# One more plain pair of gate and up in the last three feed-forward layers

## The chip, the cores and the metric

The kernel runs on one core of one Trainium2 chip. The metric is device time in microseconds (us) of one execution; lower is better. A profile of one execution shows when each engine was busy: PE multiplies matrices (PEld is its loading of the stationary operand), DVE and ACT are the two engines for elementwise work, POOL is a third that here mostly issues transfers, and SP issues the other transfers. Each engine takes its own instructions in the order in which they were written into its queue and stops at the first whose inputs are not there.

## The reference, cut to what matters

Two layers, each a half-step feed-forward network (FFN), a mixer, and a second half-step FFN. The change touches the FFN alone, and three of its four uses.

```python
def swiglu(h, w_in, w_out):
    g, u = jnp.split(h @ w_in, 2, axis=-1)
    return (jax.nn.silu(g) * u) @ w_out

for i in range(DEPTH):                       # DEPTH = 2
    h = adaln(x, norm_g[i, 0], shift[:, 0], scl[:, 0])
    x = x + HALF * gate[:, 0, None, :] * swiglu(h, ffn_w_in[i, 0], ffn_w_out[i, 0])
    ...
    h = adaln(x, norm_g[i, 2], shift[:, 2], scl[:, 2])
    x = x + HALF * gate[:, 2, None, :] * swiglu(h, ffn_w_in[i, 1], ffn_w_out[i, 1])
```

There are 512 tokens, 1024 model features and 2816 hidden features; everything is float32.

## The kernel before

All activations are kept transposed, features on 128 partitions and tokens along the row, so `x` is eight tiles of 128x512. A float32 operand is split into a high part (a copy on ACT, line 170) and a low part (a subtraction on DVE, line 171), and each product is made of three matmuls, high by high, low by high and high by low (`mm3`, lines 179 to 181).

The 2816 hidden features are 22 column blocks of 128, numbered j. For one j the kernel needs a gate block and an up block, here called a pair. There are two ways of making a pair:

- Plainly (`pair`, line 423): gate and up each take 8 slices of the model features, so 2 x 8 products over all 512 tokens. A product over 512 columns is three matmuls of 128x512, or, with the tokens in two halves (`HALVES`), six of 128x256. In halves a pair is 2 x 8 x 2 x 3 = 96 matmuls of 128x256.
- By seven products (`seven_products`, line 488), a scheme after Strassen and Winograd: the 2 x 2 arrangement of gate and up by first and second half of the features is multiplied with the 2 x 2 arrangement of features by tokens in seven products instead of eight. Each of the seven covers 4 slices of features and 256 tokens, so a pair is 7 x 4 x 3 = 84 matmuls of 128x256.

Seven products need sums of weight quarters. For each j, SP loads two quarters into a buffer `qa` (lines 500 and 501), POOL adds a third to both with an accumulating transfer (line 503, it waits for the first two), SP loads the whole gate block into `raw` (line 505) and one quarter into `a22` (line 506; the profile's page calls it `a`). DVE makes two more sums `qb` (lines 507 and 508), and then everything is split into high and low: `raw` to `whi`, `qa` to `qah`, `a22` and `qb` to `qbh`. On PE the products follow in the order a11, a12, s3, s1, a22, s2, s4; a11 and a12 use `whi`, s3 and s1 use `qah`, the last three use `qbh`. Between a11 and s1 ACT copies the first product away (`p1`, line 530; `p` on the page), because s1 is summed into the same place. DVE and ACT then put the products together (lines 536 to 543).

The seven products also need sums of the activations' quarters. `quarters` (line 326) makes them once per FFN from the normalized input, after the norm is finished: four passes on DVE, and four splits into the tiles `th` and `tl`. That takes time, so the first pairs of an FFN are made plainly from the unsummed input. In `ffn` (line 479) these are j = 0 and 1, which are worked together as soon as the norm delivers (`head_start`, PE tile `hs`), and j = 2 (line 559), whose gate weights lie in the tiles that `th` takes afterwards. From j = 3 on `seven_products` is used.

The buffers that matter: `qa` has two buffers of its own, called `own` here, and two more are made of the tiles `hhi1` and `hlo1` (line 564), which hold the first half of the features over the second half of the tokens and are read by plain pairs alone, so they come free when the last plain pair is done. The order of use is own, own, own, `hhi1`, `hlo1`, own, own, and so on. So the third j that is made by seven products takes the first one's buffer again, the fourth waits for the plain pairs. `qah` and `qal` have two buffers, `qbh` and `qbl` one.

The hidden blocks are used up in four parts, `FOUR` = 0 to 6, 6 to 12, 12 to 18 and 18 to 22: after each part the output projection (PE tile `y`) multiplies them with `ffn_w_out` and adds the result to `x`.

The code is written in the order of the computation; a scheduler at build time then fixes the order of the instructions in each engine's queue by priorities and its own estimates. The queues are static: at run time nothing overtakes within one.

Of the kernel before, what the change touches and what calls it, by code (L numbers as in the profile page):

```python
# [24 lines left out]
T = 512  # L25
# [24 lines left out]
HALVES = ((0, HT), (HT, T))  # L50
# [3 lines left out]
def decoder_kernel(ctx, tc, xT, cT, ng, adaw, adab, ffi, ffo, cwi, cw, cwo,  # L54
# [8 lines left out]
    def shift(p, n):  # L63
        p.tile([P, n // 4], F32, name="shift")
# [12 lines left out]
    def psum(name, tag="mm"):  # L77
        tag = next(six) if tag == "mm" else {"pr": "o"}.get(tag, tag)
        return ps.tile([P, T], F32, name=name, tag=tag, bufs=2)
# [35 lines left out]
    def mod(s, kind, d):  # L115
        c = s * NMOD + kind * KD + d
        return mods[:, c:c + 1]
# [65 lines left out]
    def weights(src, nk, ncol, own=None, held=3, raws=None, to=None, added=False):  # L183
        def part(name, dt, bufs, from_):
            return (from_ or wp).tile([P, nk * ncol], dt, name=name, tag=name, padded_shape=[P, KD * P], bufs=bufs)

        hi, lo = to or (part("whi", F32R, held, own), part("wlo", F32R, held, own))
        raws = raws or own
        raw = part("wraw", F32, 3 if raws in (None, wp) else 2, raws)
        nc.sync.dma_start(raw.rearrange("p (a n) -> p a n", a=src.shape[1]), src)  # L190
        if added:
            split_added(raw, src, hi, lo)
        else:
            split(raw, hi, lo)
        return [t.rearrange("p (k n) -> p k n", n=ncol) for t in (hi, lo)]


    def project(o, w, wc, h, ks, first, last, a=0, b=T):
        c = slice(wc * P, (wc + 1) * P)
        for n, (kw, k) in enumerate(ks):  # L200
            mm3(o, w[0][:, kw, c], w[1][:, kw, c], h[0][k][:, a:b], h[1][k][:, a:b],
                first and n == 0, last and n == len(ks) - 1)
# [193 lines left out]
    def ffn_in(f, j, c, own=None):  # L396
        return weights(ffi[f, j, c], KD, P, own)


    def ffn_out(f, d, m, j0, j1, own=None):  # L400
        src = ffo[f, d:d + m, :, j0 * P:j1 * P].rearrange("d p c -> p d c")
        return weights(src, m * (j1 - j0), P, own)
# [17 lines left out]
            nc.vector.tensor_mul(af, sg, u)  # L420
            self.keep(af)

    def pair(f, j, h, own=None, gate=None):
        gu = []
        for c in range(2):
            w = gate if gate and not c else ffn_in(f, j, c, own if c else None)
            o = psum("gu")
            for a, b in HALVES if gate else ((0, T),):
                project(o[:, a:b], w, 0, h, [(k, k) for k in range(KD)], True, True, a, b)
            gu.append(o)  # L430
        return gu
# [3 lines left out]
    def ffn_first(s, f, nrm, nxt, extra, ahead, first, soon, own):  # L435
        with ExitStack() as es:
# [23 lines left out]
            for p, (j0, j1) in enumerate(PARTS):  # L460
                for j in range(max(j0, nj), j1):
                    hid.activate(*pair(f, j, h, own))
                    fill()
                n = j1 - j0
                a, ka = (hid.hi[j0:j1], hid.lo[j0:j1]), [(k, k) for k in range(n)]
                last = p == len(PARTS) - 1
                for d in range(KD - 3 if last else KD):
                    w = ffn_out(f, d, 1, j0, j1, own if d % 2 else None)
                    o = psum("y")
                    project(o, w, 0, a, ka, True, True)  # L470
                    if last:
                        residual(s, d, o, nxt)
                    else:
                        fill()
                        nc.vector.scalar_tensor_tensor(x[d], o, mod(s, 2, d), x[d], op0=ALU.mult, op1=ALU.add)
# [3 lines left out]
    def ffn(s, f, nrm, nxt, w0, ahead):  # L479
        with ExitStack() as es:  # L480
            hp = pool(es, "hp", 1)
            hid = Hidden(es, 12)
            keep = hid.keep
            nj = 2
# [64 lines left out]
            with ExitStack() as tf_es:  # L549
                nrm.alloc_seven(hp, pool(tf_es, "tf", 1))  # L550
                h = nrm.hi, nrm.lo
                with ExitStack() as hw_es:
                    hw = pool(hw_es, "hw", 1)
                    shift(hw, 64)
                    w = w0 + [weights(ffi[f, j, c], KD, P, hw, 1, wp) for j, c in js[len(w0):]]

                    gate = weights(ffi[f, nj, 0], KD, P, to=[tt.tile([P, D], F32R, name="w" + e, tag=f"t{e}1") for e in "hl"])
                    os = head_start(nrm, h, [(lambda k, w=w_: (w, 0, k)) for w_ in w])
                os += pair(f, nj, h, gate=gate)
                nrm.quarters(tt)  # L560
            nj += 1
            sw_es = es.enter_context(ExitStack())

            own, quarter = (partial(swa.tile, [P, 2, KD * P // 2], F32, name="qa", bufs=2),
                            [partial(hp.tile, [P, 2, KD * P // 2], F32, name="qa", tag=t) for t in ("hhi1", "hlo1")])
            sums = chain((own, own, own), cycle((*quarter, own, own)))
            sw = pool(sw_es, "sw", 1)
            shift(sw, 64)
            for j in range(nj):
                hid.activate(os[2 * j], os[2 * j + 1])  # L570
            for p, (j0, j1) in enumerate(FOUR):
                for j in range(max(j0, nj), j1):
                    seven_products(j)
                n = j1 - j0
                a = (hid.hi[j0:j1], hid.lo[j0:j1])
                if p < len(FOUR) - 1:
                    for d in range(KD):
                        w = ffn_out(f, d, 1, j0, j1)
                        o = psum("y")
                        project(o, w, 0, a, [(k, k) for k in range(n)], True, True)  # L580
                        nc.vector.scalar_tensor_tensor(x[d], o, mod(s, 2, d), x[d], op0=ALU.mult, op1=ALU.add)  # L581
# [663 lines left out]
    ada_es.close()  # L1245
    nrm, nxt = nxt, Norm(3)
    w = ffn(2, 1, nrm, nxt, w, ffn_ahead(2))
    nrm, nxt = nxt, Norm(4)
    w = ffn(3, 2, nrm, nxt, w, lambda: nsa_in(4))
    nrm, nxt = nxt, Norm(5)  # L1250
    w = nsa(4, nrm, nxt, w, ffn_ahead(3))
    ffn(5, 3, nxt, None, w, None)


# [73 lines left out]
```

## Time and profile before

| | us |
|---|---|
| three runs | 1984.94, 1996.69, 1997.26 (median 1996.69) |
| the profiled execution, its own time | 1994.45 |
| span of the profile, first to last instruction | 1992.4 |
| DVE busy | 1471.6 (74%) |
| ACT busy | 886.4 (44%) |
| POOL busy | 212.3 (11%) |

The profiled execution's time is 2.05 us more than its span and 2.24 us under the median of the runs. The three FFNs that `ffn` makes begin their first pair by seven products at 612.79, 965.93 and 1678.08 us of the span; they are called the first, second and third FFN below. A share of busy time is an average over the whole span; what a change in one place is worth is read in that place.

### The profile page before, as it was taken

How to read it: one execution, taken by the hardware profiler on the slowest of the kernel's cores; microseconds unless marked ns; L12 is line 12 of the kernel's file. 1: busy time of each engine (PE TensorE's matmuls, PEld its weight loads, DVE VectorE, ACT ScalarE, POOL GpSimd, SP SyncE). 2: the span in 40 equal slices, each digit the busy share in tenths (PEclk: the TensorE clock that was granted, in tenths of full speed). 3: DMA queues.
4: the chain of work that ended last, by engine and by line, in shares of the span. 5: the costliest groups of instructions: out<-in, count | busy, mean ns of one | idle time of the engine just before them, and what ended most of it. 6: DMA issues, size and time to landing. Idle time of an engine off the chain costs nothing.

```text
span 1992.4 us, 32482 instructions
## 1 busy us (share of the span) xinstructions
PE 1924.9 (97%) x12644; PEld 1746.8 (88%) x12644; DVE 1471.6 (74%) x2581; ACT 886.4 (44%) x1426; POOL 212.3 (11%) x295
## 2 busy tenths in 40 slices
PE   5999999999998999999999999999999889999999
PEld 4878888898898898999989899999888789898989
DVE  7878888674467586778768677885776877786865
ACT  3322322332245353435535343456887955343532
POOL 0000000100011000000100000002354620000000
PEclk9999999999998999999999999999998999999999
DMA  8888999422236464533656553146233424665622
GB/s 310 304 317 318 329 323 331 155 98 85 89 102 186 132 175 142 155 117 96 183 135 176 142 154 117 45 139 169 66 68 76 112 64 114 172 173 156 170 69 75
DMA packets 115350, 315.78 MB, mean 158 GB/s; under 512 B 14139, under 2 KB 14411, under 8 KB 115196
## 3 DMA queue, kind: packets, MB, share of 16 engines
q1 hardware_dynamic: 97164, 274.81, 40.8%
q0 software_dynamic: 18032, 38.90, 11.5%
q8 instruction: 99, 1.62, 0.3%
q14 instruction: 55, 0.45, 0.1%
HBM read 310.51 MB, written 3.15 MB: 157 GB/s over the span
## 4 chain that ended last, share of the span: by engine, by line
PE 72%; DVE 11%; DMA 9%; ACT 5%; issue 3%; SPq 1%; DVEq 0%; ACTq 0%
PE gu L179 10%; PE gu L181 10%; PE gu L180 10%; DMA adaraw<-in_adaw 6%; PE y L179 6%; PE y L180 6%; PE y L181 6%; DVE wlo L171 2%; DVE adaraw L125 2%; PE hs L179 2%; PE hs L181 2%; PE hs L180 2%; PE cv L181 2%; PE cv L179 2%; PE cv L180 2%
## 5 line engine op out<-in xcount | busy, mean ns | idle before, releaser
L170 ACT ACTIVATE whi<-wraw 128x1024 fp32r<-128x1024 f32 (+2 forms) x271 | 268.9, 996 | 501.0 <-PE y L180 223.3
L171 DVE TENSOR_TENSOR wlo<-wraw,whi 128x1024 fp32r<-128x1024 f32 (+2 forms) x271 | 309.4, 1144 | 53.9 <-ACT whi L170 52.0
L179 PE MATMUL gu<-hhi,whi 128*128 128x256 f32 (+1 forms) x808 | 257.8, 319 | 0.0
L181 PE MATMUL gu<-hhi,wlo 128*128 128x256 f32 (+1 forms) x808 | 257.7, 319 | 0.0
L180 PE MATMUL gu<-hlo,whi 128*128 128x256 f32 (+1 forms) x808 | 257.7, 319 | 0.0
L179 PE MATMUL y<-ahi,whi 128*128 128x512 f32 x587 | 228.4, 392 | 0.8 <-ACT ahi L170 0.7
L180 PE MATMUL y<-alo,whi 128*128 128x512 f32 x587 | 227.5, 390 | 0.4 <-DVE alo L171 0.4
L181 PE MATMUL y<-ahi,wlo 128*128 128x512 f32 x587 | 227.1, 389 | 0.0
L125 DVE CUSTOM_DVE_ANT_0 adaraw<-adaraw,cond 128x1024 f32<-128x1024 f32 x144 | 174.6, 1223 | 34.6 <-DMA adaraw<-in_adaw 32.8
L179 PEld LDWEIGHTS gu<-hhi,whi 128*128 128x128 f32 x808 | 151.7, 188 | 12.3
L180 PEld LDWEIGHTS gu<-hlo,whi 128*128 128x128 f32 x808 | 151.6, 188 | 12.2
L181 PEld LDWEIGHTS gu<-hhi,wlo 128*128 128x128 f32 x808 | 151.7, 188 | 11.8
L503 POOL DMA_DIRECT2D qa<-in_ffi x57 | 68.7, 1204 | 818.5 <-DMA qa<-in_ffi 163.1
L179 PE MATMUL gu<-th,qah 128*128 128x256 f32 x456 | 129.1, 283 | 13.0 <-ACT p L530 13.0
L179 PEld LDWEIGHTS y<-ahi,whi 128*128 128x128 f32 x587 | 109.5, 188 | 27.8 <-ACT ahi L170 5.0
L180 PEld LDWEIGHTS y<-alo,whi 128*128 128x128 f32 x587 | 110.2, 188 | 24.9 <-DVE alo L171 2.5
L181 PEld LDWEIGHTS y<-ahi,wlo 128*128 128x128 f32 x587 | 110.2, 188 | 22.7
L179 PE MATMUL gu<-th,qbh 128*128 128x256 f32 x456 | 126.1, 277 | 3.2 <-ACT qbh L170 3.2
L180 PE MATMUL gu<-tl,qah 128*128 128x256 f32 x456 | 128.5, 282 | 0.0
L181 PE MATMUL gu<-th,qal 128*128 128x256 f32 x456 | 128.4, 282 | 0.0
L581 DVE SCALAR_TENSOR_TENSOR x<-y,mods,x 128x512 f32<-128x512 f32 x72 | 54.0, 750 | 98.7 <-PE y L181 98.6
L180 PE MATMUL gu<-tl,qbh 128*128 128x256 f32 x456 | 125.9, 276 | 0.0
(308 smaller groups left out, 5243.0 us busy)
## 6 DMA issues: line engine op xcount, KB each, us to landing
adaraw<-in_adaw SPq DMA_DIRECT2D x144, 512.0 KB, 5.9
wraw<-in_ffi SPq DMA_DIRECT2D x119, 512.0 KB, 4.1
qa<-in_ffi SPq DMA_DIRECT2D x114, 256.0 KB, 4.0
qa<-in_ffi POOLq DMA_DIRECT2D x57, 512.0 KB, 6.4
wraw<-in_ffo SPq DMA_DIRECT2D x72, 384.0 KB, 4.3
a<-in_ffi SPq DMA_DIRECT2D x57, 256.0 KB, 4.3
wraw<-in_cwi SPq DMA_DIRECT2D x24, 512.0 KB, 3.3
wraw<-in_nwi SPq DMA_DIRECT2D x20, 512.0 KB, 4.3
```

The source lines that it names most:

```text
L125: nc.vector.tensor_tensor_reduce(out=raw, in0=raw, in1=cond, scale=1.0, scalar=0.0, op0=ALU.mult, op1=ALU.add, accum_out=m)
L170: nc.scalar.activation(hi, src, AF.Copy)
L171: nc.vector.tensor_tensor(lo, src, hi, ALU.subtract)
L179: nc.tensor.matmul(o, sh, mh, start=first, stop=False)
L180: nc.tensor.matmul(o, sh, ml, start=False, stop=False)
L181: nc.tensor.matmul(o, sl, mh, start=False, stop=last)
L503: nc.gpsimd.dma_start(qa, bass.AP(tensor=a21.tensor, offset=a21.offset, ap=[a21.ap[0], [0, 2], a21.ap[1]]), accum_op=ALU.add)
L581: nc.vector.scalar_tensor_tensor(x[d], o, mod(s, 2, d), x[d], op0=ALU.mult, op1=ALU.add)
```

## The change

The three FFNs that `ffn` makes get a fourth plain pair. j = 3 is made by `pair`, in halves like j = 2, and is activated with the others; `seven_products` starts at j = 4, so eighteen j are made by it instead of nineteen. Nothing else is edited.

```diff
-    def pair(f, j, h, own=None, gate=None):
+    def pair(f, j, h, own=None, gate=None, halves=False):
         gu = []
         for c in range(2):
             w = gate if gate and not c else ffn_in(f, j, c, own if c else None)
             o = psum("gu")
-            for a, b in HALVES if gate else ((0, T),):
+            for a, b in HALVES if gate or halves else ((0, T),):
                 project(o[:, a:b], w, 0, h, [(k, k) for k in range(KD)], True, True, a, b)
             gu.append(o)
         return gu
...
                 os += pair(f, nj, h, gate=gate)
                 nrm.quarters(tt)
-            nj += 1
             sw_es = es.enter_context(ExitStack())
...
-            for j in range(nj):
+            for j in range(nj + 1):
                 hid.activate(os[2 * j], os[2 * j + 1])
+            hid.activate(*pair(f, nj + 1, h, halves=True))
+            nj += 2
             for p, (j0, j1) in enumerate(FOUR):
                 for j in range(max(j0, nj), j1):
                     seven_products(j)
```

The scheduler's order around this place changes with it. Numbers behind names tell buffers apart. First the queue of ACT in the first FFN, before the change, from the first j by seven products (j = 3, whose quarter is `a22_5098`) to the second (j = 4, `a22_5223`, `p1_5260`); `qa_5347` is that of the third, j = 5.

```order
L170 ACTIVATE qbh_5102<-a22_5098 128x512
L170 ACTIVATE qah_5350<-qa_5347 128x1024
L170 ACTIVATE qbh_5227<-a22_5223 128x512
L170 ACTIVATE qbh_5227<-qb_5224 128x1024
L530 ACTIVATE p1_5260<-gu_5246 128x256
```

The same queue with the change. `ahi_5208` belongs to the new plain pair, `a22_5216` and `p1_5253` to j = 4, `a22_5341` and `p1_5378` to j = 5, and `qa_5673` to j = 6.

```order
L170 ACTIVATE ahi_5208<-af_5206 128x512
L530 ACTIVATE p1_5253<-gu_5239 128x256
L170 ACTIVATE qbh_5220<-a22_5216 128x512
L170 ACTIVATE whi_5488<-wraw_5490 128x768
L170 ACTIVATE qah_5676<-qa_5673 128x1024
L170 ACTIVATE qbh_5345<-a22_5341 128x512
L170 ACTIVATE qbh_5345<-qb_5342 128x1024
L530 ACTIVATE p1_5378<-gu_5364 128x256
```

In both, the split of the third `qa` stands ahead of the second `p1`; with the change that third `qa` is the one of j = 6, a j of the next part.

Then SP's queue of transfers in the first FFN, before the change. `qa_5805` and `qa_5680` take the tiles `hlo1` and `hhi1`, `qa_5347` is the third, `a22_5098` the quarter of the first j by seven products.

```order
L190 DMA wraw_5471<-in_ffo 128x768
L500 DMA qa_5805<-in_ffi 128x512
L500 DMA qa_5680<-in_ffi 128x512
L500 DMA qa_5347<-in_ffi 128x512
L506 DMA a22_5098<-in_ffi 128x512
L506 DMA a22_5223<-in_ffi 128x512
L501 DMA qa_5347<-in_ffi 128x512
```

With the change; here `qa_5923` and `qa_5798` take `hlo1` and `hhi1`, `qa_5673` is the third, `a22_5216` the quarter of the first j by seven products.

```order
L190 DMA wraw_5464<-in_ffo 128x768
L500 DMA qa_5673<-in_ffi 128x512
L501 DMA qa_5673<-in_ffi 128x512
L190 DMA wraw_5490<-in_ffo 128x768
L500 DMA qa_6048<-in_ffi 128x512
L501 DMA qa_6048<-in_ffi 128x512
L190 DMA wraw_5516<-in_ffo 128x768
L500 DMA qa_5923<-in_ffi 128x512
L500 DMA qa_5798<-in_ffi 128x512
L506 DMA a22_5216<-in_ffi 128x512
L506 DMA a22_5341<-in_ffi 128x512
```

Both quarters of the third `qa`, two weight blocks of the output projection and one more `qa` have moved ahead of the two transfers that wait for the last plain pair; the quarters `a22` of the first and second j stay behind them. With the change the other two FFNs have the same two pieces in the same order. Elsewhere the queues differ only where neighbouring instructions have changed places, at the norms and in the mixer of the second layer.

## The prediction

> **What bounds the kernel now.** I read the page's first part, then who PE waits for, then a table of stretches cut at the pairs, and last the queues of ACT and SP at the places found. The first row is PE's busy time in the page, the other two are from the list of waits on PE (waiter, what it waited for, us in total, times, longest).
>
> ```profile
> PE 1924.9 (97%) x12644; PEld 1746.8 (88%) x12644; DVE 1471.6 (74%) x2581; ACT 886.4 (44%) x1426; POOL 212.3 (11%) x295
> ```
> ```profile
> PE gu L179 <- ACT p L530: 13.0, 4, 6.9
> ...
> PE gu L179 <- ACT qbh L170: 3.2, 2, 1.8
> ```
>
> PE bounds the kernel at 97%, so a matmul more costs its time, and time comes back only where PE stands. The longest waits inside the FFNs are for the copy `p1` and the split `qbh`, both of the seven products. Now the stretches. Columns: from:to in us, length, then busy time of PE, PEld, DVE, ACT and POOL with their counts, PE's granted clock, busy share of the DMA engines, GB/s. The first row is the plain pair j = 2 of the second FFN; then come j = 3, 4 and 5 by seven products, of the first, second and third FFN.
>
> ```profile
> 954.85:965.93 11.08, 11.08 (x97) 11.08 (x96) 9.95 (x12) 7.54 (x10) 0.00 (x0) 1.00 0.29 86
> 612.79:623.25 10.46, 10.06 (x87) 9.86 (x86) 9.05 (x12) 4.43 (x7) 2.39 (x2) 1.00 0.91 292
> 623.25:642.66 19.41, 12.52 (x87) 12.32 (x85) 9.89 (x14) 5.84 (x8) 2.39 (x2) 0.74 1.03 244
> 642.66:652.28 9.62, 9.62 (x86) 9.62 (x85) 7.55 (x10) 5.04 (x7) 1.20 (x1) 1.00 0.53 130
> 965.93:977.82 11.89, 10.08 (x87) 9.69 (x85) 6.76 (x9) 3.48 (x6) 2.41 (x2) 1.00 0.96 272
> 977.82:991.61 13.79, 11.41 (x86) 11.21 (x85) 10.21 (x14) 5.75 (x8) 2.41 (x2) 0.88 1.04 249
> 991.61:1001.13 9.52, 9.52 (x86) 9.52 (x85) 7.93 (x12) 4.93 (x7) 1.20 (x1) 1.00 0.88 249
> 1678.08:1689.55 11.47, 10.08 (x87) 9.70 (x85) 6.69 (x9) 3.52 (x5) 2.39 (x2) 1.00 0.95 271
> 1689.55:1704.40 14.85, 11.57 (x87) 11.37 (x86) 10.34 (x15) 5.74 (x8) 2.39 (x2) 0.89 1.01 234
> 1704.40:1714.02 9.62, 9.62 (x86) 9.62 (x85) 7.81 (x11) 4.94 (x7) 1.19 (x1) 1.00 0.89 258
> ```
>
> A pair by seven products takes 9.52 us when PE never stands (84 matmuls, 113.3 ns each). j = 3 and j = 4 take much more, j = 5 almost nothing: over 9.52 us the first FFN loses 0.94 + 9.89 + 0.10, the second 2.37 + 4.27 + 0, the third 1.95 + 5.33 + 0.10. That is 10.93 + 6.64 + 7.38 = 24.95 us. At the same time the DMA engines are busy for 0.91 to 1.04.
>
> j = 4 loses in two ways. In the next table each wait is followed by the stretch behind it.
>
> ```profile
> 626.07:633.12 7.05, 0.16 (x2) 0.00 (x0) 1.75 (x3) 2.84 (x5) 0.00 (x0) 0.65 1.11 252
> 633.12:638.41 5.29, 5.29 (x24) 5.29 (x25) 5.25 (x9) 1.95 (x3) 1.19 (x1) 0.50 0.93 179
> 980.54:983.08 2.54, 0.16 (x2) 0.00 (x1) 1.75 (x2) 2.49 (x4) 0.98 (x1) 1.00 1.11 256
> 983.08:987.53 4.45, 4.45 (x24) 4.45 (x25) 4.38 (x8) 1.59 (x3) 1.43 (x2) 0.62 1.09 255
> 1692.27:1695.71 3.44, 0.16 (x2) 0.00 (x0) 1.75 (x2) 2.79 (x4) 0.00 (x0) 1.00 1.11 266
> 1695.71:1700.16 4.45, 4.45 (x25) 4.45 (x25) 4.38 (x8) 1.59 (x3) 2.23 (x2) 0.62 0.86 193
> ```
>
> PE stands for 7.05, 2.54 and 3.44 us, and its next 24 matmuls then run at a granted clock of 0.50 to 0.62: 5.29, 4.45 and 4.45 us where 24 x 113.3 ns are 2.72. So 6.03 us of the loss are slow matmuls after a wait. Why PE stands is in ACT's queue, first FFN, then one row each of the second and the third.
>
> ```profile
> 617.40 0.63 ACT L170 ACTIVATE qbh<-a 128x512 fp32r<-128x512 f32 x1 [0.64 <-DMA a<-in_ffi]
> 630.28 1.06 ACT L170 ACTIVATE qah<-qa 128x1024 fp32r<-128x1024 f32 x1 [12.25 <-DMA qa<-in_ffi]
> 631.24 0.61 ACT L170 ACTIVATE qbh<-a 128x512 fp32r<-128x512 f32 x1
> 631.76 1.04 ACT L170 ACTIVATE qbh<-qb 128x1024 fp32r<-128x1024 f32 x1
> 632.71 0.36 ACT L530 ACTIVATE p<-gu 128x256 f32<-128x256 f32 x1
> 632.97 0.83 ACT L170 ACTIVATE whi<-wraw 128x768 fp32r<-128x768 f32 x1
> ```
> ```profile
> 980.24 1.06 ACT L170 ACTIVATE qah<-qa 128x1024 fp32r<-128x1024 f32 x1 [6.95 <-DMA qa<-in_ffi]
> ```
> ```profile
> 1692.87 1.06 ACT L170 ACTIVATE qah<-qa 128x1024 fp32r<-128x1024 f32 x1 [7.85 <-DMA a<-in_ffi]
> ```
>
> ACT stands at the split of j = 5's `qa`, whose transfer has not landed, and the `p1` that PE wants for j = 4 is four places behind it. That `qa` is the third: its buffer had to be given back by j = 3 first. It lands 17.49, 14.31 and 14.79 us after the start of j = 3.
>
> **The change part by part.** Write T for the end of the new plain pair, which is the start of j = 4.
>
> *The pair and the j that goes.* Per FFN 96 matmuls come and 84 go. The priced row is the plain pair above, 11.08 us (at 113.3 ns each it would be 10.88), against 9.52: +1.56 us, three times +4.68 us, all on PE's path. On ACT and DVE the pair needs two weight splits, one gate and one product with its split, less than the seven products' 4.93 us of ACT and 7.93 of DVE in 9.52; I cost them at nothing, covered by the 11.08 us of PE. Its weights are loaded and split in the places that j = 3's and j = 4's blocks had before.
>
> *The third `qa`.* It now belongs to j = 6, which comes after the output projection of part 0. Its split still stands ahead of the `p1` of j = 5 in ACT's queue. PE wants that `p1` at T + 9.52 + 2.72 = T + 12.24 (two products of 1.36 in), and it was ready 632.71 + 0.36 - 630.28 = 2.79 us after the landing, so landings up to T + 9.4 are free. Landing at the same clock time as before would be T + 6.4, T + 3.2 and T + 3.7, since T is 11.08 later than the start of j = 3 was; and SP now issues its two quarters together and ahead of the `a22` group. So the 7.05, 2.54 and 3.44 us go, and the slow matmuls with them.
>
> *The `a22` of the first j.* SP stands at the two `qa` loads that need the `hhi1` and `hlo1` tiles, and the `a22` loads are queued behind. The rows for the third FFN: SP's issues, then ACT's split of the arrived quarter, and last, over all 57, how long this transfer takes.
>
> ```profile
> 1676.80 0.95 SPq L500 DMA_DIRECT2D qa<-in_ffi  x2
> 1677.80 0.42 SPq L501 DMA_DIRECT2D qa<-in_ffi  x1
> 1678.33 0.37 SPq L500 DMA_DIRECT2D qa<-in_ffi  x1
> 1678.75 0.90 SPq L506 DMA_DIRECT2D a<-in_ffi  x2
> ```
> ```profile
> 1684.39 0.63 ACT L170 ACTIVATE qbh<-a 128x512 fp32r<-128x512 f32 x1 [2.65 <-DMA a<-in_ffi]
> ```
> ```profile
> DMA to landing us min/median/max: 2.5/4.3/11.2
> ```
>
> The first load was let go at 1676.80, 12 matmuls before the plain pairs' end, and `a22` was issued 0.67 us after that end and landed 5.64 us later, so PE got `qbh` late: that is j = 3's loss. In the new order only the two freed loads stand ahead (0.95 us), so `a22` goes at about T - 0.4. PE wants it after four products, T + 5.44, and ACT needs 0.63 before: a landing 5.2 us after the issue is free. At 5.64 us PE loses 0.43, and 0.9 for the low part on DVE; at 4.3 nothing. I take 0.5 us per FFN, 1.5.
>
> *What is left of the loss.* In the first FFN even an undisturbed j ran at 9.62; I leave 0.8 us for such slower matmuls. With 1.5 that is 2.3 of 24.95.
>
> *Transfers.* From the page's list of issues (engine, count, size, median us to landing):
>
> ```profile
> wraw<-in_ffi SPq DMA_DIRECT2D x119, 512.0 KB, 4.1
> qa<-in_ffi SPq DMA_DIRECT2D x114, 256.0 KB, 4.0
> qa<-in_ffi POOLq DMA_DIRECT2D x57, 512.0 KB, 6.4
> wraw<-in_ffo SPq DMA_DIRECT2D x72, 384.0 KB, 4.3
> a<-in_ffi SPq DMA_DIRECT2D x57, 256.0 KB, 4.3
> ```
>
> A plain pair loads 2 x 512 KB, a seven-product j 256 + 256 + 512 + 512 + 256: 768 KB less in each burst, not priced. Two weight blocks for the output projection move ahead of the waiting loads on SP; two issues take about the 0.95 us of the row above, at a time when SP would otherwise wait for PE. What stands behind the waiting loads (`a22`, later weights, POOL's sums for j = 7 and 8) is wanted after T + 5.
>
> *Sum.* 24.95 - 2.3 - 4.68 = 18.0 us. Against the profiled execution's own time 1994.45 that is 1976.5; it stands 2.24 under the median 1996.69, so against the median 1978.7. I say 1979.
>
> **A rule beside the row.** The rows show half to 0.62 of the clock behind waits of 2.54 to 7.05 us. The Trainium skill, TensorE: Matmul & The Clock Gate, Part 1, says that PE falls to half rate after an idle window of about 3.4 us and comes back after as long a busy one. By that each wait costs 1.7 us more, 5.1 us for three, where the rows give 6.03; the sum by the page would be 17.1 us. The trace agrees with the half rate and the length; that a wait of 2.54 us sufficed is the trace's, and it decides.
>
> **The rivals.**
>
> *The wait stays and moves along.* If j = 6's `qa` lands as late after T as j = 5's did after the start of j = 3, only j = 3's and j = 5's losses go, 0.94 + 2.37 + 1.95 + 0.20 = 5.46, less 4.68: 0.8 us faster, 1995.9. For it: ACT's order is unchanged. Against it: the load waits for a split on DVE that needs nothing of the new pair, and stands ahead of SP's wait.
>
> *`a22` later than thought.* Everything that waited for the plain pairs is still issued in one burst at T. If its landing takes 7.5 us, PE stands 2.3 us per FFN and pays about 2.0 for the slow clock (6.03 / 3): 24.95 - 0.8 - 4.68 - 12.9 = 6.6 us faster, 1990. From 10 us on, 4.8 + 2.0 each, the gain is gone, and at the longest seen, 11.2, it is 6.0 + 2.0 each, 24 us: 4.5 us slower, 2001. Against it: 11.2 is one of 57, and much of the old burst is now issued before T.
>
> *Nothing lost at all.* The pair at 10.88 and no loss left: 20.9 us, 1975.8.
>
> **How the numbers follow.** The waits go with only small rests (1979, including the last rival): 0.72. `a22` at 6.5 to 10 us: 0.14, about 1990. The wait moves along: 0.08, 1996. `a22` over 10 us: 0.04, 2001. Shifts elsewhere in the order that overshadow this: 0.02. The three runs lie 12.3 us apart, and the median of new ones can fall among the lower; so the likeliest case alone is 1969 to 1986, and the range that leaves out 2 in 10 is 1967 to 1991. About 1% is what a measurement of this kernel can tell from no change, and that bound, 1976.7, lies just under the forecast: of the likeliest case I give 0.34 to below it. So faster 0.34, the same 0.63, slower 0.03.
>
> **What would show it.** In the profile afterwards: PE's wait for `p` gone from the list or under 1.5 us in total; j = 4 and 5 at 9.5 to 10.3 us each with a clock of 1.00; the new pair at 10.9 to 11.1; 36 matmuls more; from the start of the new pair to the output projection about 30.9 us where before it was 39.49, 35.20 and 35.94. The prediction is wrong if ACT again stands at a `qah` ahead of `p`, if `qbh` is late by more than 1 us, or if the time comes back in a later part of the FFNs.

## The result, and the profile after

| | before | after |
|---|---|---|
| median of the runs first taken | 1994.42 us (6 runs, 1984.94 to 1997.26) | 1972.6 us (6 runs, 1968.97 to 1982.23) |
| ratio after to before | | 0.991, 95% interval 0.989 to 0.993 |
| the same pair on another chip | 1990.58 us (9 runs) | 1978.27 us (5 runs, 1975.92 to 1981.09) |
| ratio there | | 0.9938, interval 0.9922 to 0.9953 |
| profiled execution | 1994.45 us, span 1992.4 | 1970.97 us, span 1969.2 |

The kernel became faster by 21.8 us in the first comparison and by 12.3 in the second, by the medians; 18.0 had been forecast. By the intervals of the ratios the gain is 14 to 22 us in the first and 9 to 16 in the second. A difference near 1% is at the edge of what is measured here, so the two traces have to say where it comes from. First PE's line of the page after, and what PE waits for:

```profile
PE 1918.0 (97%) x12680; PEld 1739.8 (88%) x12680; DVE 1456.5 (74%) x2557; ACT 881.4 (45%) x1417; POOL 208.5 (11%) x292
```
```profile
PE y L179 <- ACT ahi L170: 2.9, 3, 1.3
...
PE gu L179 <- ACT qbh L170: 0.9, 2, 0.6
...
PE gu L181 <- DVE qbl L171: 0.5, 2, 0.2
```

There are 36 matmuls more, 12 in each of three FFNs. The wait of 13.0 us for `p` is off the list, that for `qbh` has gone from 3.2 to 0.9. New near the top is a wait at the start of an output projection, `y`. Next the stretches after, columns as before: per FFN the new pair and then the first two j by seven products.

```profile
613.10:623.98 10.88, 10.88 (x99) 10.88 (x97) 7.20 (x9) 3.92 (x5) 1.20 (x1) 1.00 0.69 173
623.98:634.87 10.89, 10.08 (x86) 9.68 (x85) 6.24 (x8) 4.12 (x6) 1.19 (x1) 1.00 1.05 324
634.87:644.39 9.52, 9.52 (x86) 9.52 (x85) 5.95 (x8) 5.04 (x7) 2.39 (x2) 1.00 0.96 225
957.26:968.14 10.88, 10.88 (x98) 10.88 (x97) 7.14 (x9) 3.68 (x5) 1.20 (x1) 1.00 0.68 187
968.14:977.66 9.52, 9.52 (x86) 9.52 (x85) 6.24 (x8) 4.23 (x6) 1.20 (x1) 1.00 1.03 316
977.66:987.18 9.52, 9.52 (x86) 9.52 (x85) 5.96 (x8) 5.04 (x7) 2.41 (x2) 1.00 0.98 255
1659.26:1670.14 10.88, 10.88 (x99) 10.88 (x97) 7.08 (x9) 3.81 (x5) 1.19 (x1) 1.00 0.70 170
1670.14:1680.88 10.74, 10.22 (x87) 9.81 (x85) 6.27 (x9) 4.12 (x6) 2.39 (x2) 1.00 1.04 312
1680.88:1690.50 9.62, 9.62 (x86) 9.62 (x85) 7.47 (x10) 5.09 (x7) 1.19 (x1) 1.00 1.05 265
```

The heads (these three stretches together) take 31.29, 29.92 and 31.24 us where j = 3, 4 and 5 took 39.49, 35.20 and 35.94: 18.18 us less. The clock is 1.00 throughout, though the DMA engines are as busy as before. ACT's queue in the first FFN, where T, the end of the new pair, is 623.98:

```profile
625.54 0.39 ACT L530 ACTIVATE p<-gu 128x256 f32<-128x256 f32 x1
629.48 0.63 ACT L170 ACTIVATE qbh<-a 128x512 fp32r<-128x512 f32 x1 [3.56 <-DMA a<-in_ffi]
630.02 0.83 ACT L170 ACTIVATE whi<-wraw 128x768 fp32r<-128x768 f32 x1
630.75 1.04 ACT L170 ACTIVATE qah<-qa 128x1024 fp32r<-128x1024 f32 x1
```

The third `qa`, for which ACT stood 12.25 us before, has landed when its split comes up. What is late instead is `a22`, the `a` in the row of 629.48. SP's row shows it issued at T - 0.43; it landed 5.9 us later:

```profile
622.70 0.80 SPq L500 DMA_DIRECT2D qa<-in_ffi  x2
623.55 1.74 SPq L506 DMA_DIRECT2D a<-in_ffi  x3
```

Two more places make up the difference of 23.2 us between the two spans. One is the end of the mixer ahead of the third FFN, from its last projections to the FFN's first matmul. Windows of before, the whole stretch and two pieces of it, and the first output projection of the first FFN; then DVE's queue of before there:

```profile
1613.40:1643.60 30.20, 25.62 (x188) 24.90 (x186) 20.05 (x56) 9.81 (x21) 2.44 (x2) 0.89 0.39 88
1625.00:1629.50 4.50, 0.97 (x6) 0.76 (x5) 1.74 (x4) 0.00 (x0) 0.00 (x0) 0.86 0.49 116
1629.50:1643.60 14.10, 13.08 (x87) 12.76 (x87) 10.37 (x36) 4.35 (x10) 0.00 (x0) 0.80 0.00 0
...
652.28:685.55 33.27, 33.00 (x147) 26.88 (x145) 19.13 (x24) 9.23 (x12) 2.41 (x2) 1.00 0.50 144
```
```profile
1627.76 0.69 DVE L507 TENSOR_TENSOR qb<-qa,wraw 128x512 f32<-128x512 f32 x1 [3.57 <-DMA wraw<-in_ffi]
1628.37 0.42 DVE L247 TENSOR_TENSOR nacc<-nacc,sq 128x256 f32<-128x256 f32 x1
```

The same places after, with the output projections of the first and the second FFN:

```profile
1600.80:1624.90 24.10, 22.91 (x188) 22.02 (x186) 19.20 (x55) 9.81 (x21) 2.44 (x2) 1.00 0.47 111
...
644.39:678.73 34.34, 32.99 (x147) 26.88 (x145) 20.52 (x27) 9.23 (x12) 2.12 (x2) 1.00 0.49 144
987.18:1021.53 34.35, 33.01 (x147) 26.88 (x145) 20.51 (x27) 9.23 (x12) 1.32 (x2) 1.00 0.53 149
```

Before, DVE waited 3.57 us for the `wraw` of a sum `qb` that belongs to j = 3 of the coming FFN, and the norm's last add, which PE wanted, stood behind it. After, no `qb` is summed that early: 30.2 has become 24.1 us, 6.1 less. The output projection after the head has become longer, 34.34 for 33.27 in the first FFN and 34.35 for 33.01 in the second, 2.4 us in all. 18.2 + 6.1 - 2.4 = 21.9; the other 1.3 us lie scattered.

The cause of the 2.4 us is in the queues of the first FFN after, ACT first and DVE second:

```profile
642.53 1.06 ACT L170 ACTIVATE qah<-qa 128x1024 fp32r<-128x1024 f32 x1 [3.22 <-DMA qa<-in_ffi]
...
649.32 0.63 ACT L170 ACTIVATE ahi<-e 128x512 fp32r<-128x512 f32 x1 [0.76 <-DVE e L542]
```
```profile
643.62 1.23 DVE L171 TENSOR_TENSOR qal<-qa,qah 128x1024 fp32r<-128x1024 f32 x1 [3.51 <-ACT qah L170]
644.77 0.69 DVE L536 TENSOR_TENSOR e<-gu,p 128x512 f32<-128x512 f32 x1
```

It is now the fourth `qa`, that of j = 7, that ACT and DVE stand at. The adds of j = 5 (L536 and on) are behind its `qal`, so `ahi` of j = 5 comes at 649.32, and PE waits 1.3 us for it. The old wait has moved along, small.

### The profile page after: what moved, and what is told of

It reads as the page before. It is cut to its first block, busy times and chain, and to the rows that moved or that the text cites. A ratio compares the mean times of both kernels' runs of the same rounds, so it can differ in the third digit from the quotient of the medians.

```text
span 1969.2 us, 32480 instructions
## 1 busy us (share of the span) xinstructions
PE 1918.0 (97%) x12680; PEld 1739.8 (88%) x12680; DVE 1456.5 (74%) x2557; ACT 881.4 (45%) x1417; POOL 208.5 (11%) x292
## 4 chain that ended last, share of the span: by engine, by line
PE 75%; DVE 9%; DMA 8%; ACT 4%; issue 2%; SPq 1%; POOL 0%; DVEq 0%; ACTq 0%
PE gu L181 10%; PE gu L179 10%; PE gu L180 10%; PE y L179 7%; PE y L180 7%; PE y L181 7%; DMA adaraw<-in_adaw 5%; PE hs L179 2%; PE hs L181 2%; PE hs L180 2%; DVE wlo L171 2%; PE cv L180 2%; PE cv L181 2%; PE cv L179 2%; DVE adaraw L125 2%
## 5 line engine op out<-in xcount | busy, mean ns | idle before, releaser
L179 PE MATMUL gu<-hhi,whi 128*128 128x256 f32 (+1 forms) x880 | 277.6, 315 | 0.0
L181 PE MATMUL gu<-hhi,wlo 128*128 128x256 f32 (+1 forms) x880 | 277.5, 315 | 0.0
L180 PE MATMUL gu<-hlo,whi 128*128 128x256 f32 (+1 forms) x880 | 277.5, 315 | 0.0
L125 DVE CUSTOM_DVE_ANT_0 adaraw<-adaraw,cond 128x1024 f32<-128x1024 f32 x144 | 174.9, 1222 | 33.9 <-DMA adaraw<-in_adaw 32.4
L180 PEld LDWEIGHTS gu<-hlo,whi 128*128 128x128 f32 x880 | 165.1, 188 | 12.3
L179 PEld LDWEIGHTS gu<-hhi,whi 128*128 128x128 f32 x880 | 165.2, 188 | 12.0
L181 PEld LDWEIGHTS gu<-hhi,wlo 128*128 128x128 f32 x880 | 165.2, 188 | 12.0
L181 PE MATMUL gu<-th,qbl 128*128 128x256 f32 x432 | 119.5, 277 | 0.5 <-DVE qbl L171 0.5
L180 PE MATMUL gu<-tl,qbh 128*128 128x256 f32 x432 | 119.3, 276 | 0.0
L179 PE MATMUL gu<-th,qah 128*128 128x256 f32 x432 | 119.2, 276 | 0.0
L180 PE MATMUL gu<-tl,qah 128*128 128x256 f32 x432 | 119.2, 276 | 0.0
```

What stands on the lines that cost most here:

```text
L125: nc.vector.tensor_tensor_reduce(out=raw, in0=raw, in1=cond, scale=1.0, scalar=0.0, op0=ALU.mult, op1=ALU.add, accum_out=m)
L179: nc.tensor.matmul(o, sh, mh, start=first, stop=False)
L180: nc.tensor.matmul(o, sh, ml, start=False, stop=False)
L181: nc.tensor.matmul(o, sl, mh, start=False, stop=last)
```

## The experiments

Each edit is against the kernel named. Times are medians, beside the kernel before on the same chip.

**The third `qa` without its adding transfer** (of before; what is left out: a21 isn't added to that `qa`):

```diff
-                nc.gpsimd.dma_start(qa, bass.AP(tensor=a21.tensor, ...
+                if j != 5: nc.gpsimd.dma_start(qa, bass.AP(tensor=a21.tensor, ...
```

> The kernel before, nineteen seven-product j; left out is the adding transfer of the third seven-product j of the last three FFNs (a21 is not added to its qa: 3 transfers of 57). Theory (PE stands because ACT waits for the third qa with p1 queued behind it): in the trace of before the two plain quarters of this qa had landed by 619.99, when the adding transfer was issued, and the sum landed at 630.28; without it the split can go at about 620, so PE's waits of 7.05, 2.54 and 3.44 us go, and the 6.03 us of slow matmuls behind them. The stretch of j = 4 falls from 19.41, 13.79 and 14.85 to 9.5 to 10.5 us in all three FFNs, in sum about 19 us less, time about 1975 against 1994. Rival (j = 4 is late for its other operands, or for the crowd on the DMA engines as a whole): taking out one 512 KB transfer of some six shortens the waits by a part only; stretches of 12 us and more stay, time 1986 or above.

Measured: 1971.31 us against 1994.58, ratio 0.9876 (0.9847 to 0.9906). ACT's split of that `qa` in the first FFN, and the stretches of j = 4:

```profile
622.95 1.06 ACT L170 ACTIVATE qah<-qa 128x1024 fp32r<-128x1024 f32 x1 [0.79 <-DMA qa<-in_ffi]
```
```profile
626.91:636.43 9.52, 9.52 (x86) 9.52 (x85) 7.53 (x11) 5.04 (x7) 1.19 (x1) 1.00 1.04 240
969.72:979.24 9.52, 9.52 (x87) 9.52 (x86) 8.74 (x12) 5.04 (x7) 2.41 (x2) 1.00 1.09 239
1675.25:1684.77 9.52, 9.52 (x86) 9.52 (x85) 6.76 (x10) 5.04 (x7) 2.39 (x2) 1.00 1.08 250
```

The split goes 7.1 us after the start of j = 3 (615.87) instead of 17.49, and j = 4 loses nothing, with the DMA engines busy for 1.04 to 1.09. The crowd of transfers as such doesn't hold PE up; this one landing did. The profiled execution took 1974.51 us, as expected (about 1975); the median lies 3 us lower, within the spread of the four runs (1965.9 to 1975.19).

**One buffer for `qah` and `qal`** (of before): the late transfer stays, its place in ACT's queue changes.

```diff
-                ah_, al_ = (sw.tile([P, 2, QT], F32R, name=f"qa{e}", bufs=2) for e in "hl")
+                ah_, al_ = (sw.tile([P, 2, QT], F32R, name=f"qa{e}", bufs=1) for e in "hl")
```

> The kernel before (three plain pairs, nineteen by seven products), but with one buffer in place of two for the split quarters qah and qal. The split of the third seven-product j then cannot go before PE has used the second one's, so in ACT's order it stands behind the p1 of j = 4 instead of ahead of it; transfers, their number and their buffers are as before. Theory (the loss is the place in ACT's queue, not the late transfer as such): the third qa lands as late as before, 14 to 18 us after the start of j = 3, but nothing that j = 4 needs is behind it, and PE wants it only 2.7 us into j = 5, at about 11 + 9.5 + 2.7 = 23 us. The stretch of j = 4 falls from 19.41, 13.79 and 14.85 to 9.5 to 10.6 us, some 17 to 19 us in all: 1976 to 1978 against 1994. Rival 1 (the crowd on the DMA engines holds back other operands of j = 4 too): j = 4 stays at 12 us and more, 1986 or above. Rival 2 (single buffers make the split of every j late): j = 4 falls, but the undisturbed j rise from 9.52 by 0.2 to 0.5 us in 57 places, 11 to 28 us: 1987 to 2005.

Measured: 1968.91 us against 1991.98, ratio 0.9896 (0.9853 to 0.9939). ACT in the first FFN (j = 3 starts at 616.44) and j = 4 in the three FFNs:

```profile
628.22 0.37 ACT L530 ACTIVATE p<-gu 128x256 f32<-128x256 f32 x1
...
633.52 1.07 ACT L170 ACTIVATE qah<-qa 128x1024 fp32r<-128x1024 f32 x1 [2.43 <-DMA qa<-in_ffi]
```
```profile
626.64:636.16 9.52, 9.52 (x86) 9.52 (x85) 6.43 (x10) 5.05 (x7) 1.19 (x1) 1.00 1.03 242
...
968.96:978.48 9.52, 9.52 (x86) 9.52 (x85) 8.73 (x12) 5.04 (x7) 3.61 (x3) 1.00 1.10 287
1667.25:1676.77 9.52, 9.52 (x87) 9.52 (x85) 8.73 (x12) 5.04 (x7) 3.58 (x3) 1.00 1.09 288
```

This `qa` lands 17.1 us after the start of j = 3, as late as before, and now nobody minds, because `p` of j = 4 has gone 5 us ahead of it. That settles the cause: a late operand in an in-order queue, ahead of one that is wanted sooner. And the whole gain of the change is had without a fourth pair. The kernel became 23.1 us faster where 17 to 19 were expected. The trace shows where the rest may lie: the mixer's end took 24.1 us here too (`qb` stands ahead of the norm's add as before, but its transfer was there in time), and j = 3 took 32.5 us over the three FFNs where it had taken 33.8.

**More time, no transfer more or less** (of before): the matmuls of the third plain pair are made twice.

```diff
-            for a, b in HALVES if gate else ((0, T),):
+            for a, b in HALVES * 2 if gate else ((0, T),):
```

> The kernel before, three plain pairs and nineteen seven-product j, with each matmul of the third plain pair made twice (96 matmuls more in each of the last three FFNs, no transfer more or less). It asks whether the cure is the 10.9 us of PE work put before the first seven-product j, or the transfers saved and the third qa moved into the next part. Theory (time alone): 3 x 10.88 = 32.6 us come, of the loss of 24.95 about 22 go: stretches of j = 3, 4, 5 at 9.5 to 11 us each, time about 1994.4 + 32.6 - 22 = 2005. Rival (it is the saved transfers or the part that the third qa belongs to): j = 4 still takes 13 to 19 us in the three FFNs, time 2020 to 2027.

Measured: 2019.83 us against 1994.58, ratio 1.0127 (1.0107 to 1.0147). j = 3 and 4 in the first and third FFN; then SP's rows with the third `qa` and with `a22`, and ACT's split of `a22`:

```profile
628.62:645.04 16.42, 12.99 (x86) 12.57 (x85) 6.87 (x9) 4.17 (x6) 2.39 (x2) 0.79 1.03 267
645.04:654.56 9.52, 9.52 (x86) 9.52 (x85) 8.36 (x12) 5.04 (x7) 1.19 (x1) 1.00 0.85 242
...
1702.68:1718.53 15.85, 11.48 (x87) 11.05 (x86) 6.50 (x8) 4.17 (x6) 2.39 (x2) 0.89 1.04 261
1718.53:1728.05 9.52, 9.52 (x87) 9.52 (x86) 8.73 (x12) 5.04 (x7) 1.19 (x1) 1.00 0.86 249
```
```profile
622.52 0.33 SPq L500 DMA_DIRECT2D qa<-in_ffi  x1
...
628.30 2.88 SPq L506 DMA_DIRECT2D a<-in_ffi  x3
```
```profile
636.97 0.63 ACT L170 ACTIVATE qbh<-a 128x512 fp32r<-128x512 f32 x1 [6.40 <-DMA a<-in_ffi]
```

Neither expectation was right as a whole. j = 4 is cured with no transfer saved and with the third `qa` in the same part as before. But time is not all that differs: the scheduler's order on SP has moved here too, and the third `qa` is issued at 622.52, 6.1 us ahead of the end of the pairs (628.62), where in the kernel before it came after that end. And j = 3 got worse and lost 6.3 to 6.9 us in each FFN: `a22` was issued 0.3 us before the end of the pairs, much as in the changed kernel, and took 8.7 us, where it took 5.9 there; the quarters of three `qa` had been asked for in the 6 us before. That is the rival "`a22` later than thought", and its price. So 10.9 us more of PE work doesn't by itself bring what the change brings. In the changed kernel the third `qa` goes 10.7 us ahead of the end of the pairs; that the crowd just ahead of `a22` is what delayed it here is read from the order of the issues and wasn't tried alone.

**The change in one FFN alone**, the third or the first:

```diff
-            hid.activate(*pair(f, nj + 1, h, halves=True))
-            nj += 2
+            if f == 3:
+                hid.activate(*pair(f, nj + 1, h, halves=True))
+                nj += 1
+            nj += 1
```

> The change in the third of the three FFNs alone; first and second as before. Heads: from the start of the new pair to the output projection 31.2 us in the third, against 35.94, so 4.7 less; first and second keep 39.5 and 35.2. Besides, the change ran 4.9 us faster at the end of the mixer ahead of the third FFN, where before the norm's last add stood on DVE behind a prefetched qb that waited for its transfer. Theory A (that place is tied to the third FFN's own prefetch): both go here, 9.6 less, about 1984.8. Theory B (the place depends on an accident of the order far ahead, or of the transfers): only the head, about 1989.7, and PE's wait for the norm's add of about 3.5 us is there.

> The change in the first of the three FFNs alone; second and third as before. Head: 31.3 us from the new pair to the output projection against 39.49, 8.2 less; second and third keep 35.2 and 35.9. Theory A (the mixer's end is tied to the third FFN's prefetch): PE's wait for the norm's add at the mixer's end stays at about 3.5 us, time about 1994.4 - 8.2 = 1986. Theory B: it goes here too, about 1981. With the second FFN by difference (5.3 less) the three single changes must add up to the 23 us of the profiled pair of runs, if they don't act on one another.

Measured: third alone 1985.04 against 1994.58, ratio 0.9957 (0.9938 to 0.9976); first alone 1987.75, ratio 0.9963 (0.9946 to 0.998). That is 9.5 and 6.8 us, theory A in both. The changed heads took 10.88 + 10.80 + 9.62 = 31.3 us in the third and 10.88 + 10.60 + 9.62 = 31.1 in the first. The mixer's end took 24.1 us with the third alone, and with the first alone PE waited 3.2 us there for the norm's add. The sum of both is 16.4; with the 5.3 us of the second FFN's head, which wasn't run alone, it makes 21.7 of the 21.8. That this comes out so closely is luck: each of the two ratios has an interval some 7 us wide, and the other pair of medians gave 12.3.

**The sum `qb` on POOL** (of before, first seven-product j of the third FFN):

```diff
-                nc.vector.tensor_tensor(qb[:, 0], qa[:, 1], raw[:, 0], ALU.add)
+                (nc.gpsimd if (f, j) == (3, 3) else nc.vector).tensor_tensor(qb[:, 0], qa[:, 1], raw[:, 0], ALU.add)
...
```

> The kernel before; the two adds that make qb of the first seven-product j of the third FFN are moved from DVE to POOL, nothing else. Theory (at the mixer's end the norm's last add stands in DVE's queue behind this qb, which waits for its transfer): PE's wait for the norm's add falls from 3.5 us to under 1, the slow clock behind it goes, and the stretch from the last group of the mixer's output projection to the third FFN's first matmul is 24.1 us as with the change, against 30.2: 4 to 6 us less, 1989 to 1990.5 against 1994.5. Rival (the add is late for the mixer itself, and qb only happened to stand there): PE's wait of 2.6 to 4 us stays, time within 1 us of before.

Measured: 1991.03 us against 1991.98, ratio 0.9995 (0.9977 to 1.0014): no difference that can be measured. PE's wait for the norm's add is gone, but the mixer's end takes 26.2 us, not 24.1. POOL's rows there, and DVE's:

```profile
1626.50 1.28 POOL L507 TENSOR_TENSOR qb<-qa,wraw 128x512 f32<-128x512 f32 x1 [8.39 <-DVE rs_b L217]
1627.86 1.40 POOL L508 TENSOR_TENSOR qb<-qb,wraw 128x512 f32<-128x512 f32 x1
```
```profile
1625.99 0.15 DVE L216 SCALAR_TENSOR_TENSOR rs_a<-rs_r 128x2 f32<-128x2 f32 x1
...
1626.57 1.23 DVE L216 SCALAR_TENSOR_TENSOR rs_a<-rs_r 128x2 f32<-128x2 f32 x1
1627.72 0.41 DVE L247 TENSOR_TENSOR nacc<-nacc,sq 128x256 f32<-128x256 f32 x1
1628.06 1.22 DVE L217 TENSOR_TENSOR rs_b<-rs_a,nv 128x2 f32<-128x2 f32 x1
```

The adds met the norm's short chain on DVE: two steps of 128x2 elements, 0.15 us otherwise, took 1.23 and 1.22 and ended with POOL's adds. 2.1 us of the cure were lost so. The theory was right on the wait and wrong on the time; the rival had the time and not the wait. The wait itself also varies: with the `qb` in the same place, DVE stood 3.57 us in the trace of before, 2.94 with the first FFN alone changed, and 0.17 with single buffers. Over the traces of all these kernels, the mixer's end takes 24.1 to 30.2 us in the seven where `qb` stands on DVE ahead of the norm's add, and 23.9 to 24.4 in the six with a fourth pair in the third FFN, where none does. So of the 6.1 us between the two traces of before and after, what a usual run gets is less, and how much stays open.

**`a22` early** (of the changed kernel), into a tile that is free then:

```diff
-                a22 = tmp("a22")
+                a22 = tmp("a22") if j > nj else None
...
-                e = sw.tile([P, 4, HT], F32, name="e")
+                e = sw.tile([P, 4, HT], F32, name="e"); a22 = a22 if j > nj else e[:, 0:2].rearrange("p a b -> p (a b)")
```

> The changed kernel; the a22 of the first seven-product j is loaded into the tile e, which is free at that time, so that its issue on SP stands ahead of the two loads that wait for the plain pairs' end. Theory (the 1.37 and 1.22 us that PE still loses at the first seven-product j are a22 issued 0.4 us before the end of the pairs and landing 5 to 6 us later): both go, that j takes 9.5 us in all three FFNs, 2.7 us less, about 1970 against 1972.6. Rival (the splits on ACT or DVE are late anyway, or another load takes the late place): the stretch stays at 10.3 us or more, time as with the change.

Measured: 1970.58 us against 1991.98, ratio 0.9898 (0.9861 to 0.9936). The first seven-product j takes 9.52 us in all three FFNs, as expected; the first of them, and the output projections of the first and the third:

```profile
625.93:635.45 9.52, 9.52 (x87) 9.52 (x85) 5.55 (x7) 3.71 (x5) 2.39 (x2) 1.00 1.00 314
...
644.97:678.11 33.14, 32.98 (x147) 26.88 (x145) 19.36 (x25) 9.23 (x12) 1.96 (x2) 1.00 0.47 143
...
1689.01:1723.65 34.64, 33.03 (x146) 26.88 (x145) 20.78 (x27) 9.22 (x12) 2.07 (x2) 1.00 0.49 144
```

So the rests in the heads were `a22`. But in the third FFN, where PE no longer waits for `a22`, it comes 1.2 us sooner to the wait behind the fourth `qa`, and the projection went from 33.01 to 34.64. In the first FFN it went the other way, from 34.34 to 33.14; over the three FFNs the projections are 0.4 us longer. Some 2 us are left by the medians, which doesn't stand out of the runs' spread.

**A fifth plain pair** (of the changed kernel):

```diff
-            hid.activate(*pair(f, nj + 1, h, halves=True))
-            nj += 2
+            for j in (nj + 1, nj + 2):
+                hid.activate(*pair(f, j, h, halves=True))
+            nj += 3
```

> The changed kernel with one plain pair more, five and seventeen, in each of the last three FFNs. Theory (with four the loss is gone but for the a22, which is tied to the end of the plain pairs and not to their number): the fifth pair costs 10.88 - 9.52 = 1.36 us in each FFN, 4.1 in all, and the rests of 0 to 1.4 us stay: 1976 to 1977.5, about 4 slower than the change. Rival (four pairs cover the loss only in part, or the transfers saved matter further on): the same as the change or faster, 1970 to 1973.

Measured: 1973.39 us against 1991.98, ratio 0.9903 (0.9871 to 0.9934): the same as the change, so the rival was right. The rest at the first seven-product j is gone (9.52 us in all three FFNs), and so is the wait in the output projections (32.9 us each). Two plain pairs and one j are 10.88 + 10.88 + 9.52 = 31.28 us, where the changed kernel took 31.29, 29.92 and 31.24: the further pair costs 4.1 us in the three FFNs, and covers 2.6 us in the heads and 3.0 in the projections (34.34 + 34.35 + 33.01 against 98.7).

**Both causes removed, and single buffers with the change.** Four kernels on one chip: the changed one again; before with single buffers and the early `a22`; the changed one with single buffers; before with single buffers again. The edits are those shown above.

> The changed kernel once more, beside the next three on the same chip. Expected 1971 to 1975 against about 1993 for the kernel before, with the three heads at 10.9 + 9.5 to 10.9 + 9.5 us again.

> The kernel before with three plain pairs, with one buffer for the split quarters and the first a22 loaded early into e; no plain pair added. Theory (two causes explain all of the loss in the heads: the split of the late third qa ahead of p1, and the late a22): j = 3, 4 and 5 take 9.5 us each in all three FFNs, 28.6 us a head; single buffers alone left 10.20, 11.57 and 10.71 for j = 3, so 3.9 us less than that, 1965 against 1968.9. Rival (as with the early a22 in the changed kernel, part comes back as PE waits for the last j's split at the start of part 0's output projection): heads at 28.6, but 1 to 1.5 us more behind each, 1967 to 1969.

> The changed kernel (four plain pairs) with one buffer for the split quarters. Theory (the change gains nothing but the removal of the wait behind the third qa): where that wait is gone already the fourth pair only costs its matmuls, 1.36 us in each FFN, 4.1 in all, less what the a22 is late with three pairs and not with four (3.9 against 2.6 us): 1.5 to 4 us slower than single buffers with three pairs (1968.9), that is 1970.5 to 1973. Rival (the transfers saved or the later start of the seven products help elsewhere too): faster than single buffers with three pairs by 2 us or more, 1967 or less.

> One buffer for the split quarters in the kernel before, once more, for the comparison with the two above on one chip. Expected 1967 to 1971.

| kernel | median, us | ratio to before | interval |
|---|---|---|---|
| changed, again | 1978.27 | 0.9938 | 0.9922 to 0.9953 |
| three pairs, single, early `a22` | 1971.38 | 0.9907 | 0.989 to 0.9925 |
| four pairs, single | 1968.28 | 0.9891 | 0.9872 to 0.9909 |
| three pairs, single | 1971.31 | 0.9912 | 0.989 to 0.9935 |

All kernels with single buffers were faster than the change here, by 7 to 10 us; for four pairs the interval lies apart from the change's, for the other two it overlaps at the edge. Among the three nothing stands out. Of the times expected, three pairs with single buffers came nearest (1967 to 1971). The changed kernel and the one with the early `a22` were slower than expected by theory or rival, and the one with four pairs lay between the two. With four pairs and single buffers every j of the heads takes 9.52 us and every output projection 33.0; the extra matmuls (4.1 us) are paid by the late `a22` that three pairs don't cover, and the profiled spans are equal, 1967.8 us. So my theory that the pair only costs there fell: it costs what it covers. With the early `a22` the heads got 3 us shorter than with single buffers alone, but in that trace the `qb` at the mixer's end waited again and PE with it, 3.6 us. Nor do the two causes explain all of the loss in the heads: j = 3 of the first FFN still took 10.46 us, as before. PE waits 0.41 us there for `p` of j = 3, as it did before (0.40); on ACT that copy stands behind the `ahi` of a plain pair, which waits for DVE. The changed kernel's repeat shows the heads of its first trace (the six j by seven products take 59.7 us against 59.8), and output projections of 35.3, 34.1 and 33.9 us, longer by 1.7 us in all: part of why it was slower on this chip.

## Why the prediction was right, point by point

- *The pair and the j that goes.* Sized at 11.08 us from the only plain pair in halves that the trace had; the new one takes 10.88 in all three FFNs, the lower bound. 3 x 1.36 = 4.08 us instead of 4.68.
- *The third `qa`.* The cause was right, and is shown by two experiments that leave the pairs alone: make it land early, or take it out from ahead of `p1`, and j = 4 takes 9.52 us. One detail was for the most part wrong: I wrote that it is late because its buffer must first be given back. SP did stand for that in the kernel before, but shortly: 1.0, 0.3 and 0.2 us in the three FFNs, for DVE's `qal` of j = 3. The rest is the queue and the transfer: in the order of before, its first quarter stands on SP behind two loads that wait for the end of the plain pairs, and its adding transfer, issued from 619.99 on, took some 10 us, until ACT could start at 630.28. In the changed kernel its quarters go 10.7 and 10.3 us ahead of T, and the adding transfer, issued at 617.70, takes 6.3 us: the sum is there at T, where T + 6.4 had been reckoned with.
- *The slow clock.* It went with the waits: 1.00 in all nine stretches. The Trainium skill, TensorE: Matmul & The Clock Gate, Part 1, gives an idle window of about 3.4 us for the drop to half rate. The runs here don't bear it out as a bound on a single wait: the clock fell after a wait of 1.94 us (below).
- *`a22`.* Issued at T - 0.43 (T - 0.4 forecast). 1.37, 0 and 1.22 us were lost with 0.10 elsewhere, 2.7 in all, where 1.5 and 0.8 of rest had been taken, 2.3. The rival that it lands much later was no idle one: in the kernel with the matmuls made twice it did, at 6.3 to 6.9 us in each FFN.
- *The sum in the heads.* 24.95 - 2.69 - 4.08 = 18.18, against 18.0. It is so close partly by luck: the pairs cost 0.6 us less than reckoned and the rests 0.4 us more.
- *What the sum lacked.* Two terms of opposite sign. The wait that moves along, a rival priced whole, came in part: 2.4 us in the projections, at the fourth `qa`. And the mixer's end, 6.1 us in the profiled pair, had been put under shifts of the order elsewhere, with a chance of 0.02; it is a shift that the order does show, since with the change no `qb` of the coming FFN is summed ahead of the norm. That is more than the neighbouring instructions that I had seen change places there.
- *The signs.* The wait for `p`, the clock, the new pair and the 36 matmuls came as named. j = 4 took 10.89 us in the first FFN and 10.74 in the third, above the 9.5 to 10.3 named, and 2.4 us came back in a later part of the FFNs, which had been named as a sign against the prediction; it is small beside 18.2.
- *1979 against 1972.6 and 1978.27.* Both medians lie in the range. 1979 started from a median of 1996.69; from the 1994.42 of six runs the same 18.0 gives 1976.4. The gain is 1.1% and 0.6% by the medians, and 0.9% and 0.6% by the ratios, so it stands at or under the bound of about 1%, as the 0.34 and 0.63 had it; both intervals leave out no gain at all. 18.0 us lies within the first interval and above the second. The projections, longer by 1.7 us, explain a part of that; the rest stays open.

## What to carry to other kernels

When an engine that executes in order stands at an operand that is late, look first at what is queued behind it and wanted sooner: changing the order (here one buffer fewer) gave as much as hiding the transfer behind more work, and took no extra matmul. A prefetched operation that may wait for its transfer shouldn't stand ahead of the last step of a serial chain, as the sum `qb` stood ahead of the norm's add; what that cost here went from nothing to 6 us from kernel to kernel. And when a wait is covered, look for the next one in the same queues, since it comes up sooner by what was gained.

## What the hardware showed that I had not expected

*A wait of 2 us was enough for the clock to fall.* In the traces of all these kernels PE waits 0.9 us or more ahead of a seven-product j's `qa` or `qb` 21 times. I took the time of the 24 matmuls behind each wait. After the eight waits of 0.90 to 1.84 us they took 3.11 to 3.35 us; after the thirteen of 1.94 to 6.89 us they took 4.05 to 5.59, against 2.72 undisturbed. One stretch from each side of the step, after 1.84 us in the kernel without the adding transfer, and after 1.94 in that with the third FFN alone:

```profile
965.24:968.36 3.12, 3.12 (x25) 2.92 (x26) 1.89 (x2) 0.89 (x1) 1.20 (x1) 1.00 0.89 314
```
```profile
981.13:985.77 4.64, 4.63 (x25) 4.44 (x25) 0.68 (x1) 0.00 (x0) 1.20 (x1) 0.65 1.05 293
```

Both are the wait for `qbh` of the first seven-product j of the second FFN. The granted clock is 1.00 in the one and 0.65 in the other. A tenth of a us more of waiting went with 1.5 us of slow matmuls; whether something else differs between the two, such as the moment at which the wait began, wasn't tried.

*Small steps on DVE stood while POOL added.* The rows of the sum on POOL above: DVE's steps with two SBUF inputs grew from 0.15 to 1.23 us while POOL added. POOL's second add, beginning while DVE's `nacc` add ran, took 1.40 us for 1.28, a single case. The Trainium skill, SBUF — State Buffer, Who interferes with whom, says that a DVE instruction with two SBUF inputs contends with a GpSimd one (POOL here) that reads SBUF, because the second input comes through a read interface that the two share. The trace agrees for DVE's steps, with these numbers.
